# Seven early pieces, prefetched compression weights, full transposes and an output block's first half begun early, in a hybrid attention and RWKV-7 layer on one core

## The chip, the cores and the metric

The kernel runs on one core of one Trainium2 chip. The metric is device time of one execution in microseconds (us), from outside the program; less is better. TensorE (PE) does the matmuls, VectorE (DVE), ScalarE (ACT) and GpSimd (POOL) the elementwise work, SyncE (SP) issues nearly all DMA transfers, in one queue and in program order.

## What is computed

One decoder layer over 256 tokens of width 2048 in float32. The reference, cut to what matters:

```python
hn = rms_norm(h, pre_norm_g)
proj = hn @ w_in                       # 2048 -> q, kv6, gates, z_a, feat_b, z_b
o_a = nsa_mixer(q, k_cmp, v_cmp, k_slc, v_slc, k_win, v_win, gates, ...)
o_b = rwkv7_mixer(feat_b, mu, w0, w2, a0, a2, k_k, k_a, r_k, ln_w, ln_b)
mix = concat([o_a * silu(z_a), o_b * silu(z_b)])
h = h + rms_norm(mix @ w_out, post_norm_g)
# in nsa_mixer: kc = silu(blocks(k_cmp) @ cmp_k_w1) @ cmp_k_w2, the same for v; softmax branches
# in rwkv7_mixer: a recurrence over time with a 64 x 64 state for each of 16 heads, y normalized by head
```

## The kernel before, in words

**Split matmuls.** Every weight is loaded as float32 (SP), rounded to a high part H (ACT, L287), and the rest is kept as a low part L (DVE, L288). A product is three matmuls: H with the high and the low part of the activations, L with the high part. The helper `mm` (L154) issues every matmul and `transpose` (L167) every transpose, so these two lines stand for all of PE's work. Four raw buffers, four H and three L hold the weights on their way.

**Pieces.** The input projection is 57 feature-major pieces, f0 to f56, of 128 output features each: f0 is the low-rank input, then 12 pieces of RWKV half 0 (heads 0 to 7), 8 of keys and values, 12 of RWKV half 1, 8 queries and 16 z. A piece is two halves (f60 and f61 are the halves of piece 6) of 24 matmuls of 128x256. `N_FIRST` = 4 pieces are begun together while x arrives; the pieces from there to `N_EARLY` take a bank of `banks`; from then on each takes one of the two banks of `ppool`. Before the first query stand the token-major pieces, t00 to t15 (`token_major`): two groups w of 96 matmuls of 128x268, each with two PSUM banks `pts`, which ACT empties (L1138, L1139). The output projection has four blocks n of 512 columns and eight pieces j each; a piece o{n}{j} is 12 matmuls of 128x512, for two token halves i. Pieces j = 0 to 3 (the A part) need mixA, the attention's result; j = 4 to 7 (the B part) need mixB, the RWKV result. PSUM has 8 banks: 2 in `ppool`, 6 in `banks`, which all other work shares.

**Order.** The program is written by generators in lanes (chain, rwkv, blk0, blk1, nsa0, nsa1, gate). After each piece `progress` runs every generator that is due by a clock that counts PE's columns (`now`); `yield 9.0` says that the next step is due 9 us of matmuls later. `pick` runs lanes until a buffer is free. The tile scheduler then orders each engine's instructions, with priorities by kind (`level`).

**Steps touched.** `row_statistics` gives the row norm as a broadcast tile `rbc` (matmul `arena,small` 128x256, copy L455); every piece's evacuation (L537) needs it, and the 128x384 matmul after it makes the attention bias rows. `compress` multiplies blocks of keys and values by eight chunks of the compression weights of 512 KB (SP L943, L947), each loaded one chunk ahead; its matmuls are those of 128x32. `solve` inverts 32x32 triangles on DVE (L737, L739), sends the result through DRAM (`zs`, `zt`, L745 to L766) and uses it in the 32x32 matmuls after `yield 9.0`. The chain of a half then runs four steps c over 64 tokens: matmuls `VS,GR` and `AR`, a copy on ACT (L824), matmuls 64x64 with the inverse, a copy on DVE (L834), and matmuls for y and the next state; y goes out by ACT (L878). At its end y is normalized (L888 to L894), transposed by eight sets of four 64x64 transposes for both halves, and added to mixB's input by L904. `out_part` computes a part of an output block; the A parts of n = 0 to 2 (`NA` = 3) go out to y2 by ACT (L1249), and the B part is added to that. Block 3 runs all eight pieces at the end:

```python
    for n in range(NA):
        pts = out_part(n, range(4), ppool if n % 2 == 0 else banks)
...
    until(lambda: not any(lanes.values()))
...
    for n in range(4):
        js = list(range(4, 8) if n < NA else range(8))
```

Of the kernel before, what the change touches and what calls it, by code (L numbers as in the profile page):

```python
# [14 lines left out]
ALU = mybir.AluOpType  # L15
# [41 lines left out]
N_EARLY = 6  # L57
# [15 lines left out]
GLAT = 1.5  # L73

# [45 lines left out]
def hybrid_block(ctx: ExitStack, tc: tile.TileContext, xT, xtok, wfm, wtm, wout, vecs, gpost, lora, table,  # L120
# [44 lines left out]
    def transpose(o, i, idn):  # L165
        now[0] += 0.11
        PE.transpose(out=o, in_=i, identity=idn)  # L167
# [132 lines left out]
    for n, j in [(n, j) for n in range(NA) for j in range(4)] + [  # L300
            (n, j) for n in range(4) for j in range(4 if n < NA else 0, 8)]:
        queue.append((wout[n, j], [P, 2, 512], f"o{n}{j}_"))
# [410 lines left out]
    def solve(hb):  # L713
# [53 lines left out]
        yield 9.0  # L767
# [129 lines left out]
        for i in range(4):  # L897
            m = 4 * hb + i
            q0 = 64 * (i % 2)
            ytp = yield from bank()  # L900
            for c in range(4):
                o = T * c + P * (i // 2)
                transpose(ytp[:, 64 * c:64 * c + 64], ysb[q0:q0 + 64, o:o + P], ident[q0:q0 + 64, q0:q0 + 64])
            DVE.scalar_tensor_tensor(mix[1][:, m, :], ytp[:, :T], vcol(V_LNW, m), mix[1][:, m, :], op0=ALU.mult,  # L904
                                     op1=ALU.add)
            ytp.free(2.0)
            yield 0.5
# [15 lines left out]

    def compress(a, nm):
        if a == 0:
            pace(SP.dma_start(post, pos), marks[-2])
            pace(SP.dma_start(w2t, cw2), marks[-2])
        blks = yield from sb(4)
# [9 lines left out]
        w1n = None  # L938
        for hf in range(4):
            w1 = w1n  # L940
            if w1 is None:
                w1 = yield from sb(4)
                pace(SP.dma_start(w1[:], cw1[a, :, 8 * hf:8 * hf + 8, :].rearrange("p j d -> p (j d)")), marks[-2])  # L943
                yield 3.0
            if hf < 3:
                w1n = yield from sb(4)
                pace(SP.dma_start(w1n[:], cw1[a, :, 8 * hf + 8:8 * hf + 16, :].rearrange("p j d -> p (j d)")),  # L947
                     marks[-1])
            for j in range(2):
                for q in range(4):  # L950
                    jj = 4 * j + q
                    mm(cps[32 * q:32 * q + 32, 0:P], blk[:, 8 * hf + jj].rearrange("p g i -> p (g i)"),
                       w1[:, jj * P:jj * P + P], start=hf == 0 and j == 0, stop=hf == 3 and j == 1)
            w1.free(1.0)
            yield 2.0
# [162 lines left out]
    def token_major():  # L1118
        VV = N_.VV = pick(arena, 4).ap.rearrange("p (w i t) -> p w i t", w=2, i=2)
        for w in range(2):  # L1120
            pts = [pick(ppool, 1) for i in range(2)]
# [112 lines left out]
    def out_part(n, js, pool, order=None):  # L1234
        pts = [pick(pool, 1) for i in range(2)]
        for pair in order or [[j] for j in js]:
            hl = [take() for j in pair]
            for i in range(2):
                with at("proj"):
                    for j, (H, L) in zip(pair, hl):  # L1240
                        out_mms(pts[i][:], i, H, L, j, j == js[0], j == js[-1])
            progress()
        return pts

    for n in range(NA):
        pts = out_part(n, range(4), ppool if n % 2 == 0 else banks)
        with at("evac"):
            for i in range(2):
                ACT.activation(y2[:, i, 512 * n:512 * n + 512], pts[i][:], AF.Copy)  # L1249
                pts[i].free(1.0)  # L1250
    until(lambda: not any(lanes.values()))
# [46 lines left out]
    for n in range(4):  # L1298
        js = list(range(4, 8) if n < NA else range(8))
# [6 lines left out]
        pts = out_part(n, js, ppool if n % 2 == 0 else banks, order)  # L1306
# [85 lines left out]
```

## Time and profile before

| | before |
|---|---|
| time, median of 3 runs | 577.52 us (576.17 to 577.62) |
| profiled execution, its own time | 575.76 us |
| its span, first to last instruction | 574.0 us |
| PE busy | 557.3 us (97%), 4812 matmuls |
| weight loads (PEld) | 519.4 us (90%) |
| DVE busy | 426.7 us (74%) |
| ACT busy | 311.8 us (54%) |
| POOL busy | 55.8 us (10%) |
| mean granted clock of TensorE | 0.996 |
| moved by DMA | 99.97 MB, mean 174 GB/s |

The span lies inside the execution's own time; 1.76 us lie around it. A duration in a row of the timeline is from the start of the first instruction to the end of the last; matmuls overlap, so the time that one costs is the distance between two starts. "Idle before" names what the engine waited for last.

### The profile page before, as it was taken

Reading aid. Unit: us, or ns where it says so; the run is one execution under the profiler, and the core shown is the slowest. Engines: PE = TensorE matmul, PEld = TensorE weight load, DVE = VectorE, ACT = ScalarE, POOL = GpSimd, SP = SyncE. Lnnn points to the kernel's source line nnn. Section 1 sums busy time; section 2 is a strip of 40 time slices with the busy share of each in tenths; the row PEclk is TensorE's granted clock in tenths of the full one; section 3 lists DMA queues with packets and bytes.
Section 4 is the critical chain, followed back from the end, with each engine's and each line's share of the span. In section 5 each row is a group of like instructions: output and inputs, shape, how many; then the busy total and the mean of one; then the engine's idle time right before and its main releaser. Section 6 shows DMA issues by size and latency. Waiting matters only on the chain.

```text
span 574.0 us, 12180 instructions
## 1 busy us (share of the span) xinstructions
PE 557.3 (97%) x4812; PEld 519.4 (90%) x4812; DVE 426.7 (74%) x892; ACT 311.8 (54%) x566; POOL 55.8 (10%) x95
## 2 busy tenths in 40 slices
PE   9999999999999999999999999999999999999994
PEld 8998999998989999999988999999999987777883
DVE  5888997867988666569789369899766473576855
ACT  6858764623445434457675468566633353564632
POOL 3202300400000000141031000000000000000002
PEclk9999999999999999999999999999999999999998
DMA  8967444557675844333346253356634455674723
GB/s 293 367 199 248 148 163 140 189 156 237 215 268 154 214 145 148 121 114 104 99 138 212 95 156 120 120 167 209 186 114 146 136 158 188 185 293 153 227 90 147
DMA packets 41365, 99.97 MB, mean 174 GB/s; under 512 B 14395, under 2 KB 17116, under 8 KB 40924
## 3 DMA queue, kind: packets, MB, share of 16 engines
q1 hardware_dynamic: 41020, 98.88, 53.2%
q8 instruction: 38, 0.62, 0.5%
q10 hardware_dynamic: 288, 0.31, 0.2%
q14 instruction: 19, 0.16, 0.1%
HBM read 93.93 MB, written 5.24 MB: 173 GB/s over the span
## 4 chain that ended last, share of the span: by engine, by line
PE 78%; DMA 7%; DVE 5%; ACT 4%; issue 2%; SPq 1%; POOL 1%; DVEq 0%; ACTq 0%
PE banks L154 76%; PE banks L167 2%; DMA arena<-in_cw_dram 2%; DMA us<-GR 1%; DMA arena<-us 1%; DMA rf__96<-in_wfm_dram 1%; DMA rf__2334<-in_wfm_dram 1%; DMA zs<-arena 1%; DMA arena<-zt 1%; DVE y L1289 0%; SPq L724 0%; DVE small L537 0%; ACT arena L1036 0%; ACT L892 0%; POOL arena L627 0%
## 5 line engine op out<-in xcount | busy, mean ns | idle before, releaser
L154 PE MATMUL banks<-arena 128*32 128x128 f32 (+3 forms) x470 | 32.3, 255 | 2.1 <-POOL arena L269 1.1
L154 PEld LDWEIGHTS banks<-arena 128*32 128x32 f32 (+3 forms) x470 | 26.6, 137 | 5.7 <-DMA arena<-in_cw_dram 1.5
L737 DVE TENSOR_TENSOR arena<-arena 64x31 f32<-64x31 f32 (+15 forms) x62 | 20.5, 330 | 8.0 <-DMA arena<-us 7.3
L539 ACT ACTIVATE small<-small 128x256 f32<-128x256 f32 x25 | 12.4, 503 | 17.2 <-DVE small L537 17.1
L739 DVE TENSOR_TENSOR arena<-arena 64x31 f32<-64x31 f32 (+15 forms) x62 | 20.4, 330 | 0.8
L167 PE MATMUL banks<-small,arena 128*128 128x128 f32 (+1 forms) x112 | 16.8, 263 | 0.1
L1094 ACT ACTIVATE arena<-arena 128x256 f32<-128x256 f32 x16 | 6.6, 415 | 18.2 <-DVE arena L1208 15.0
L154 PE MATMUL banks<-AR,arena 64*128 64x128 f32 x128 | 15.4, 289 | 0.0
L154 PEld LDWEIGHTS banks<-AR,arena 64*128 64x128 f32 x128 | 12.2, 187 | 2.4 <-issue 0.5
L167 PEld LDWEIGHTS banks<-small,arena 128*128 128x128 f32 (+1 forms) x112 | 11.8, 139 | 2.6 <-issue 1.1
L594 DVE RECIPROCAL arena<-arena 128x256 f32<-128x256 f32 x8 | 13.8, 1739 | 0.4 <-ACT arena L591 0.2
L1036 ACT ACTIVATE arena<-arena,mx 128x128 f32<-128x128 f32 (+1 forms) x32 | 14.1, 442 | 0.0
L627 POOL TENSOR_SCALAR arena<-arena,small 128x256 f32<-128x256 f32 x8 | 9.8, 1220 | 42.7 <-DVE small L537 34.9
L624 POOL TENSOR_SCALAR arena<-arena 128x256 f32<-128x256 f32 x8 | 9.5, 1187 | 38.8 <-ACT arena L623 37.6
L540 DVE SCALAR_TENSOR_TENSOR arena<-small 128x256 f32<-128x256 f32 x25 | 11.8, 481 | 1.9 <-ACT small L539 1.9
L1293 POOL TENSOR_TENSOR y<-y,xres 128x512 f32<-128x512 f32 x2 | 2.9, 1454 | 101.5 <-ACT y L1292 101.5
L154 PE MATMUL banks<-VS,GR 128*64 128x64 f32 x256 | 11.4, 228 | 0.0
L154 PEld LDWEIGHTS banks<-VS,GR 128*64 128x64 f32 x256 | 9.5, 137 | 1.8 <-issue 0.7
L687 DVE TENSOR_TENSOR GR<-banks,small 128x1024 f32<-128x1024 f32 x8 | 9.8, 1221 | 0.9 <-PE banks L154 0.9
L537 DVE TENSOR_TENSOR small<-banks,small 128x256 f32<-128x256 f32 x25 | 10.3, 417 | 0.2
L1032 DVE CUSTOM_DVE_ANT_0 arena<-banks,arena 128x128 f32<-128x128 f32 (+1 forms) x32 | 10.1, 348 | 0.0
L864 POOL TENSOR_TENSOR arena<-arena,PC 128x256 f32<-128x256 f32 x4 | 2.7, 685 | 71.5 <-DVE arena L854 36.3
(1375 smaller groups left out, 2143.4 us busy)
## 6 DMA issues: line engine op xcount, KB each, us to landing
arena<-in_cw_dram SPq DMA_DIRECT2D x8, 512.0 KB, 4.7
arena<-in_wfm_dram SPq DMA_DIRECT2D x4, 512.0 KB, 8.9
xres<-in_xtok_dram SPq DMA_DIRECT2D x2, 1024.0 KB, 7.5
xr<-in_xT_dram SPq DMA_DIRECT2D x3, 512.0 KB, 7.2
bscr<-arena SPq DMA_DIRECT2D x1, 1536.0 KB
out_dram<-y SPq DMA_DIRECT2D x5, 256.0 KB, 2.3
arena<-bscr SPq DMA_DIRECT2D x8, 128.0 KB, 3.2
gpt<-in_gpost_dram SPq DMA_DIRECT2D x1, 1024.0 KB, 5.0
```

What stands on the lines that cost most here:

```text
L154: last[0] = PE.matmul(o, lhsT, rhs, **kw)
L167: PE.transpose(out=o, in_=i, identity=idn)
L537: DVE.tensor_tensor(f[:, 1:T + 1], pt[:, :T], rbc, op=ALU.mult)
L539: ACT.activation(tm, f[:, 0:T], AF.Copy, scale=vcol(V_MU, c))
L540: DVE.scalar_tensor_tensor(o, f[:, 1:T + 1], omu[:, c:c + 1], tm, op0=ALU.mult, op1=ALU.add)
L594: pace(DVE.reciprocal(A.nrm[i + j], A.nrm[i + j]))
L627: POOL.tensor_scalar(fk[:], ta[:], ka2[:, m:m + 1], ka1[:, m:m + 1], op0=ALU.mult, op1=ALU.add)
L687: DVE.tensor_tensor(A.GR[:, i].rearrange("p h c t -> p (h c) t"), gp.ap.rearrange("p h (c t) -> p (h c) t", c=4), gmask[:, None, :].to_bro ...
L737: DVE.tensor_tensor(t_, U[:, 0:j, j:j + 1].to_broadcast([64, j, w]), Z[:, j:j + 1, j:32].to_broadcast([64, j, w]), op=ALU.mult)
L739: DVE.tensor_tensor(Z[:, 0:j, j:32], Z[:, 0:j, j:32], t_, op=ALU.add)
L1032: DVE.tensor_tensor_reduce(out=dst, in0=src, in1=bb, scale=1.0, scalar=-3.0e38, op0=ALU.add, op1=ALU.max, accum_out=mx[:, i, j:j + 1])
L1036: ACT.activation(dst, dst, AF.Exp, bias=mx[:, i, j:j + 1], accum_out=sm[:, i, j:j + 1])
```

## The change

1. `N_EARLY` goes from 6 to 7: piece 6 takes a bank of `banks` too and may begin before the row statistics are done.
2. The compression weights are fetched by `fetch_cw`, up to two chunks ahead of the one in use, if four arena units and twelve in all are free; each step yields `CWLAT` = 2.5 in place of 3.0 and 2.0.
3. `yield 9.0` before the 32x32 matmuls of `solve` becomes `yield 11.0`.
4. y is transposed by four sets of four 128x128 transposes (two sets for each half) in place of eight sets of 64x64; two instructions per set (now L908) read the bank with a stride.
5. A group of token-major pieces takes one bank of `ppool` and one of `banks`, in place of both of `ppool`.
6. The order of the output weights is: the A parts of all four blocks, then the B parts. The A parts of n = 1 and 2 run in `banks`; that of n = 3 runs in `ppool` and stays there (`held`) until its B part is added at the end, in the same accumulation. All other B parts run in `banks`.

The diff, with the lines that only follow left out:

```diff
-N_EARLY = 6
+N_EARLY = 7
...
+CWLAT = 2.5
...
-    for n, j in [(n, j) for n in range(NA) for j in range(4)] + [
-            (n, j) for n in range(4) for j in range(4 if n < NA else 0, 8)]:
+    for n, j in [(n, j) for js in (range(4), range(4, 8)) for n in range(4) for j in js]:
         queue.append((wout[n, j], [P, 2, 512], f"o{n}{j}_"))
...
-        yield 9.0
+        yield 11.0
         t2p = yield from bank2()
...
-        for i in range(4):
-            m = 4 * hb + i
-            q0 = 64 * (i % 2)
+        for a in range(2):
+
             ytp = yield from bank()
             for c in range(4):
-                o = T * c + P * (i // 2)
-                transpose(ytp[:, 64 * c:64 * c + 64], ysb[q0:q0 + 64, o:o + P], ident[q0:q0 + 64, q0:q0 + 64])
-            DVE.scalar_tensor_tensor(mix[1][:, m, :], ytp[:, :T], vcol(V_LNW, m), mix[1][:, m, :], op0=ALU.mult,
-                                     op1=ALU.add)
+                o = T * c + P * a
+                transpose(ytp[:, P * c:P * c + P], ysb[:, o:o + P], ident)
+            ytv = ytp.ap.rearrange("p (c b t) -> p c b t", c=4, b=2)
+            for b in range(2):
+                m = 4 * hb + 2 * a + b
+                mv = mix[1][:, m, :].rearrange("p (c t) -> p c t", c=4)
+                DVE.scalar_tensor_tensor(mv, ytv[:, :, b, :], vcol(V_LNW, m), mv, op0=ALU.mult, op1=ALU.add)
...
+    cws, cwn = {}, [0]
+
+    def fetch_cw(upto, must):
+
+        while cwn[0] < upto and arena.find(4) is not None and (must or arena.busy.count(False) >= 12):
+            n = cwn[0]
+            cws[n] = arena.take(4)
+            cwn[0] += 1
+            pace(SP.dma_start(cws[n][:], cw1[n // 4, :, 8 * (n % 4):8 * (n % 4) + 8, :].rearrange("p j d -> p (j d)")),
+                 marks[-2])
...
+            fetch_cw(2, False)
...
+            n = 4 * a + hf
+            fetch_cw(min(n + 3, 8), False)
+            if n not in cws:
+                yield lambda: arena.find(4) is not None
+                fetch_cw(n + 1, True)
+                yield 4.0
+            w1 = cws.pop(n)
...
-            yield 2.0
+            yield CWLAT
...
-            pts = [pick(ppool, 1) for i in range(2)]
+            pts = [pick(pool, 1) for pool in (ppool, banks)]
...
-    def out_part(n, js, pool, order=None):
-        pts = [pick(pool, 1) for i in range(2)]
+    def out_part(n, js, pool, order=None, begun=None):
+        pts = begun or [pick(pool, 1) for i in range(2)]
...
-                        out_mms(pts[i][:], i, H, L, j, j == js[0], j == js[-1])
+                        out_mms(pts[i][:], i, H, L, j, not begun and j == js[0], n < NA and j == js[-1] or j == 7)
...
-        pts = out_part(n, range(4), ppool if n % 2 == 0 else banks)
+        pts = out_part(n, range(4), ppool if n == 0 else banks)
...
+    held = out_part(NA, range(4), ppool)
     until(lambda: not any(lanes.values()))
...
-        js = list(range(4, 8) if n < NA else range(8))
+        js = list(range(4, 8))
...
-        pts = out_part(n, js, ppool if n % 2 == 0 else banks, order)
+        pts = out_part(n, js, banks, order, held if n == NA else None)
```

In the program as it is built, `mm` is now L156, `transpose` L169, the casts L289 and L290, the copies of the chain L825 and L835, y's way out L879.

**On PE, at the row statistics.** Names: hf51 and lf51 are the H and L parts of the second half of piece 5; `arena,small` 128x256 is the broadcast of `rbc`, 128x384 the bias rows. Before:

```order
L154 MATMUL banks_74<-xH_76,lf51__475 128x256 x8
L154 MATMUL banks_74<-arena_73,small_72 128x256
L154 MATMUL banks_74<-arena_73,small_72 128x384
L154 MATMUL banks_74<-xH_76,hf60__506 128x256
L154 MATMUL banks_74<-xL_75,hf60__506 128x256
```

Of the change:

```order
L156 MATMUL banks_74<-xH_76,lf51__475 128x256 x8
L156 MATMUL banks_74<-xH_76,hf60__506 128x256
L156 MATMUL banks_74<-xL_75,hf60__506 128x256
...
L156 MATMUL banks_74<-arena_73,small_72 128x256
...
L156 MATMUL banks_74<-xH_76,lf60__505 128x256 x8
L156 MATMUL banks_74<-xH_76,hf61__547 128x256
...
L156 MATMUL banks_74<-arena_73,small_72 128x384
```

Twelve matmuls of f60 now stand ahead of the broadcast, and the rest of f60 and twelve of f61 between it and the 128x384.

**On SP, at the compression weights.** `in_cw1` is a chunk of them, rf180 the raw weights of the first half of piece 18, `us0` the way of `solve` through DRAM. Before:

```order
L943 DMA arena_73<-in_cw1_dram 128x1024
L279 DMA rf180__1492<-in_wfm_dram 128x1024
L279 DMA rf181__1540<-in_wfm_dram 128x1024
L279 DMA rf190__1581<-in_wfm_dram 128x1024
L947 DMA arena_73<-in_cw1_dram 128x1024
L724 DMA us0_1522<-GR0_742 32x16x32 x4
L279 DMA rf191__1629<-in_wfm_dram 128x1024
L730 DMA arena_73<-us0_1522 64x1024
L947 DMA arena_73<-in_cw1_dram 128x1024
```

Of the change:

```order
L281 DMA rf180__1519<-in_wfm_dram 128x1024
L935 DMA arena_73<-in_cw1_dram 128x1024
L281 DMA rf181__1561<-in_wfm_dram 128x1024
L935 DMA arena_73<-in_cw1_dram 128x1024
L281 DMA rf190__1604<-in_wfm_dram 128x1024
L281 DMA rf191__1648<-in_wfm_dram 128x1024
L935 DMA arena_73<-in_cw1_dram 128x1024 x2
L725 DMA us0_1502<-GR0_742 32x16x32 x4
L935 DMA arena_73<-in_cw1_dram 128x1024
```

The second chunk's load moves ahead from behind rf190 to behind rf181, and the third, fourth and fifth are issued by the time at which the third was.

**On PE, at the end of the A parts.** ho13 and lo13 are the last A piece of n = 1, `arena` 64x64 the product with the inverse in step c = 3 of half 1, which L824 (L825) must have copied for and which L834 (L835) copies out. Before:

```order
L154 MATMUL banks_74<-VS1_3330,GR1_3329 64x64 x8
L154 MATMUL banks_74<-arena_73,AR1_3328 64x128 x4
L154 MATMUL banks_74<-ho10__5821,mixA_5769 128x512 x4
...
L154 MATMUL banks_74<-ho13__5925,mixA_5769 128x512 x3
L154 MATMUL banks_74<-arena_73 64x64 x8
L154 MATMUL banks_74<-ho13__5925,mixA_5769 128x512
```

Of the change:

```order
L156 MATMUL banks_74<-ho13__5904,mixA_5734 128x512 x4
L156 MATMUL banks_74<-lo13__5903,mixA_5734 128x512 x2
L156 MATMUL banks_74<-VS1_3348,GR1_3347 64x64 x8
L156 MATMUL banks_74<-arena_73,AR1_3346 64x128 x4
L156 MATMUL banks_74<-arena_73 64x64 x8
L156 MATMUL banks_74<-VS1_3348,GR1_3347 64x64 x8
L156 MATMUL banks_74<-arena_73,AR1_3346 64x128 x4
L156 MATMUL banks_74<-ho20__5935,mixA_5734 128x512 x4
```

Before, 21 output matmuls stood between the chain's AR matmuls and the 64x64 that needs their result, and others behind it; now the three chain steps follow each other directly.

## Rows read from the trace of the kernel before

**Rows 1.** Waits of PE: line waited for, us in total, times, longest.
```profile
PE banks L154 <- ACT small L1139: 2.5, 2, 1.4
...
PE banks L154 <- DMA arena<-in_cw_dram: 1.0, 1, 1.0
PE banks L154 <- DMA arena<-zt: 0.7, 1, 0.7
```

**Rows 2.** The page: busy time of the engines, landing of the compression weights' loads.
```profile
PE 557.3 (97%) x4812; PEld 519.4 (90%) x4812; DVE 426.7 (74%) x892; ACT 311.8 (54%) x566; POOL 55.8 (10%) x95
...
arena<-in_cw_dram SPq DMA_DIRECT2D x8, 512.0 KB, 4.7
```

**Rows 3.** Busy time in stretches: us; PE, PEld, DVE, ACT, POOL busy; clock; DMA.
```profile
60.00:80.00 20.00, 19.89 (x172) 19.52 (x171) 19.77 (x35) 14.46 (x23) 4.32 (x6) 1.00 0.44 149
...
566.00:574.00 8.00, 0.00 (x0) 0.00 (x0) 4.46 (x8) 1.51 (x4) 1.47 (x1) 0.72 0.57 213
```

**Rows 4.** Timeline of PE and DVE at the row statistics: start, us, engine, line.
```profile
42.42 0.59 PE L154 MATMUL banks<-arena,small 128*128 128x256 f32 x2
44.23 0.59 PE L154 MATMUL banks<-arena,small 33*128 33x384 f32 x1 [1.22 <-DVE small L455]
...
43.76 0.42 DVE L455 COPY small<-banks 128x256 f32<-128x256 f32 x1
```

**Rows 5.** Timeline of PE at the first wait for compression weights.
```profile
132.66 0.75 PE L154 MATMUL banks<-xH,lf__1460 128*128 128x256 f32 x5
134.41 0.43 PE L154 MATMUL banks<-arena 128*32 128x128 f32 x8 [0.99 <-DMA arena<-in_cw_dram]
```

**Rows 6.** Timeline of SP and PE from half 0's inverse to its first use.
```profile
183.83 0.47 SPq L745 DMA_DIRECT2D zs<-arena  x1
...
195.45 1.43 SPq L766 DMA_DIRECT2D arena<-zt  x3
...
197.74 0.24 PE L154 MATMUL banks<-arena,GR 32*32 32x32 f32 x2 [0.67 <-DMA arena<-zt]
```

**Rows 7.** Timeline of PE at the first wait of the token-major pieces.
```profile
292.42 0.28 PE L154 MATMUL banks<-KCL,qh 128*128 128x256 f32 x1
293.87 0.39 PE L154 MATMUL banks<-ht__3305,xH 128*128 128x268 f32 x1 [1.17 <-ACT small L1139]
```

**Rows 8.** Timeline of PE at the first output piece.
```profile
468.22 0.50 PE L154 MATMUL banks<-ho__5627,mixA 128*128 128x512 f32 x1
469.38 0.83 PE L154 MATMUL banks<-ho__5627,mixA 128*128 128x512 f32 x2 [0.66 <-DVE arena L1208]
```

**Rows 9.** Timeline of PE: one set of 64x64 transposes, one of 128x128, what follows.
```profile
511.48 0.46 PE L167 MATMUL banks<-small,arena 64*128 64x64 f32 x4
511.87 1.20 PE L154 MATMUL banks<-ho__6059,mixB 128*128 128x512 f32 x4
...
305.83 0.60 PE L167 MATMUL banks<-small,arena 128*128 128x128 f32 x4
306.36 1.16 PE L154 MATMUL banks<-AR,arena 64*128 64x128 f32 x16
```

**Rows 10.** Timeline of PE, ACT and DVE: one chain step of half 1 among output pieces.
```profile
488.55 0.66 PE L154 MATMUL banks<-arena,AR 128*64 128x128 f32 x8
489.14 1.19 PE L154 MATMUL banks<-ho__5821,mixA 128*128 128x512 f32 x4
...
494.12 0.73 PE L154 MATMUL banks<-arena 64*64 64x64 f32 x16
494.78 0.50 PE L154 MATMUL banks<-ho__5925,mixA 128*128 128x512 f32 x1
...
489.29 0.39 ACT L824 ACTIVATE arena<-banks 128x256 f32<-128x256 f32 x1 [2.80 <-PE banks L154]
491.79 1.06 ACT L287 ACTIVATE ho__5983<-ro__5980 128x1024 fp32r<-128x1024 f32 x1 [0.36 <-PE banks L154]
...
494.89 0.68 DVE L834 COPY VS<-banks 64x512 f32<-64x512 f32 x1
```

More of the change, by code (lines that the diff above doesn't have):

```diff
@@ L937, in compress @@
         cps = yield from bank()
-        w1n = None
         for hf in range(4):
[L940 to L948, printed above, removed]
+            n = 4 * a + hf
[5 more added lines that the diff above has]
+            w1 = cws.pop(n)
             for j in range(2):
```

## The prediction

> **What bounds the kernel now.** I read the page first: PE is busy 557.3 us of a span of 574.0, no other engine over 427 [rows 2]. So the time is PE's work plus the places where PE stands. The stretches come next: the last 8 us hold no matmul [rows 3], and that tail (norm, product and way out of the last block) is not touched. This leaves 574.0 - 557.3 - 8.0 = 8.7 us in which PE stands between its first and its last matmul. The list of waits then says for whom: 2.5 us for ACT's emptying of the token-major banks, 1.0 for compression weights, 0.7 for the reads of zt [rows 1], 1.2 for the copy of rbc [rows 4], 0.7 before the first output piece [rows 8]; about 2.6 us are small and have no name there. The timelines give the size of each place, because a wait costs more than its idle time: the five matmuls ahead of the compression take 0.75 us, one alone 0.28 [rows 5, 7], so they follow each other every (0.75 - 0.28)/4 = 0.12 us. By that step the sixth would have started at 133.26, and it started at 134.41: 1.15 us lost, where 0.99 are called idle. I add 0.16 us for each wait. An output matmul of 128x512 steps by (1.20 - 0.50)/3 = 0.23 us [rows 8, 9].
>
> So the change can win by taking waits away (7 us at most, with these additions) or by taking work from PE, and it can lose by making new waits. DVE matters wherever it is full: from 60 to 80 us it is busy 19.77 of 20 us while PE is busy 19.89 [rows 3].
>
> **The change part by part.**
>
> *Seventh early piece.* Before, PE goes straight from the broadcast to the 128x384 and waits 1.22 us for L455, which DVE finishes at 43.76 + 0.42 [rows 4]. Now 12 matmuls of f60 (1.44 us) stand ahead of the broadcast and 24 others (2.9 us) between it and the 128x384, more than the wait. Gain 1.22 + 0.16 = 1.4 us. What is late next: rbc itself, by up to 1.4 us, and every L537 behind it on DVE. These empty the piece banks, and with a seventh piece six of the six banks are taken at that moment (two of the first four pieces, three early ones, the one of the statistics). DVE has a quarter of a microsecond to spare from 60 to 80, so the other end is 0.
>
> *Compression weights.* A load of a chunk lands after 4.7 us [rows 2]; it was issued one chunk ahead and PE waited at the first [rows 5]. Now the second chunk is issued right behind the first piece of raw weights that follows the first chunk, and three more a little later. Gain 1.15 us, I take 1.2 with the small second place. The chunks are passed by none that PE waits for: on SP the raw weights rf190 and rf191 and the way of `solve` (us0) now stand behind one or two chunks more, issues of about half a microsecond each [rows 6]; at the other end one of them is late by one load and the gain is 0.
>
> *The inverse of `solve`.* zs is issued at 183.83 and the product starts at 197.74, 13.9 us later, behind reads of zt that are issued until 196.9 [rows 6]. The later yield moves the product from the second half of f27 to the first of f30. But zs too is now issued later: it stood behind raw load rf280 with the product in f271, it now stands behind rf301 with the product in f300. Raw loads run ahead of PE by a fixed number of buffers, so in both orders the distance is one half-piece less than that lead, and the wait stays. I take 0; ends are -0.9 us (gone) and +0.7 (doubled).
>
> *Token-major pieces.* Group w = 1 began when ACT had emptied both banks of w = 0, and the first query when it had emptied w = 1: two waits, 2.5 us [rows 1], the first of 1.17 [rows 7]. With a bank of each kind, each next user finds a free one, and the emptying has a whole group of 96 matmuls (11.5 us) to hide under. Gain 2.5 + 2 x 0.16 = 2.8 us. For it all others have one bank fewer of six for two groups; RWKV half 1 and the heads behind it move later and press on DVE there. Bound from the nearest row: one such wait comes back, 1.5 us; the other end is 2.8.
>
> *First output piece.* It loses 469.38 - 468.22 - 0.23 = 0.93 us, waiting for the last head's work on DVE [rows 8]. In the new order two more sets of 64x64 matmuls of the chain stand ahead of it, 0.66 us each, from 494.12 to 494.78 [rows 10]. The splits of mixA still end last, so I take 0.6; ends 0 and 0.9.
>
> *Full transposes.* A set of four 64x64 takes 0.39 us to the next matmul, one of four 128x128 takes 0.53 [rows 9]. Eight of the first are 3.1 us, four of the second 2.1: at least 1.0, at most 1.5 if the large ones step like the small. I take 1.2. L908 reads as many elements with a stride; it follows PE and hides under output matmuls.
> By the Trainium skill, TensorEngine Tiling (Array Packing), Key Properties, different tiles "can execute LdWeights and Matmul in parallel". By that rule the small transposes, which alternate between the two halves of the partitions, would overlap and the full ones would win nothing; the sum below would be 1.2 us smaller. The row speaks against it: four small ones take 0.39 us, 0.10 each, one behind the other [rows 9].
>
> *Order of the output parts.* The A part of block 3 only moves: 4 x 12 matmuls, 11 us, from the end to ahead of the first B matmul, where they cover half 1's norm and gate. No wait there is in the list now, so the gain is 0. The norm of y had 42 output matmuls as cover before its first transposes and has 36 now, 8.3 us; it had no wait, so the cost is 0, at the other end the 6 matmuls, 1.4 us.
>
> *A new wait.* At the end of block 1's A part the chain's AR, the 64x64 and VS,GR now follow each other with nothing between. The step as it ran before: AR at 488.55, the next matmul at 489.14, L824 from 489.29 for 0.39 [rows 10]. The 64x64 can start at about 489.7, so PE stands 0.6 us. The 64x64 take until 494.78, L834 runs from 494.89 for 0.68, so VS,GR waits until 495.6: 0.8 us more. Cost 1.4 us. ACT also has a weight cast of 1.06 us in its queue [rows 10]; if that and a half of its like on DVE are in the way, it is 3.2. It can hardly be less than 1.2.
>
> Sum: -1.4 - 1.2 + 0 - 2.8 - 0.6 - 1.2 + 1.4 = -5.8 us. The profiled execution took 575.76 us (span 574.0 and 1.76 around it) and would take 570.0. It lies 1.76 us under the median of the runs, 577.52, so the median should come to **571.7**.
>
> **The rivals.**
> *All waits go.* zt's wait too (0.9), the first piece's whole (0.3 more), transposes at 1.5, the new wait at 1.2, and half of the 2.6 us without a name: -5.8 - 0.9 - 0.3 - 0.3 - 0.2 - 1.3 = -8.8, 568.7 us. For it: PE has nothing else to wait for. Against it: the distance of zs.
> *DVE gives it back.* The gain at 44 us returns as waits for L537 (1.4), one token-major wait returns further down (1.5), the new wait is 3.2 (1.8 more): -5.8 + 4.7 = -1.1, 576.4 us. For it: DVE is full from 60 to 80 us. Against it: PE is full there as well, so it carries the load.
> *Slower: the chain of half 1 runs in the open.* It ran beside the last projection pieces and now falls deeper into the A parts, with three steps c there. If each of them, not only the last, waits for its two copies at the upper price of 3.2 us, that is 9.6 in place of 1.4: -5.8 + 8.2 = +2.4, 579.9 us. It decides at the point where the copies L825 stand behind a cast that itself waits for its raw load. Against it: in the new order output matmuls stand between the steps of c = 1 and c = 2.
> *Part of the change does nothing.* Full transposes win nothing because small ones overlap: 572.9.
>
> **How the numbers follow.** The forecast has a chance of 0.55; all waits gone 0.15; DVE gives back 0.18; the open chain 0.08; no gain by the transposes 0.04. A measurement of this kernel can tell 0.3%, 1.7 us, from no change: faster is under 575.8, slower over 579.3. Faster holds the forecast, the first rival, the last and a third of the second: 0.80; same the rest of the second: 0.12; slower 0.08. The range reaches from 568.0, a little under the best case, to 576.5, at the second rival; above it lie the open chain and a part of the second.
>
> **What would show it.** In the list of waits L455, in_cw and L1139 are gone and zt stays. Output matmuls at the end of block 1 show two idle gaps, one behind the copy L825 and one behind L835, 0.6 and 0.8 us. L169 has 16 fewer transposes and PE's busy time falls by about 1 us. The tail stays at 8 us. I am wrong if PE shows waits for L537 between 45 and 80 us, if RWKV or the heads wait for a bank from 280 us on, or if PE stands before the first B matmul.

## The result, and the profile after

The changed kernel takes **571.64 us** (median of 4 runs, 571.08 to 572.24); before, in the same session, 577.48 (576.17 to 577.62). The ratio is 0.9904, with a 95% interval of 0.9886 to 0.9923: faster by about 1%, some 5.5 us. The profiled execution is the shortest of the four, 571.08 us, with a span of 569.3. One execution further down, the profiled one of e9, ran at a granted clock of 0.85 from end to end; its lengths are not used.

The page of the kernel after, busy time of the engines:

```profile
PE 552.2 (97%) x4796; PEld 519.2 (91%) x4796; DVE 426.8 (75%) x892; ACT 311.1 (55%) x566; POOL 57.2 (10%) x95
```

PE's busy time fell by 5.1 us [rows 2], far more than the 1 us that I had ascribed to the transposes, though in this execution part of PE's work ran slower than before. The list of waits of PE after (line waited for; us in total, times, longest), beside [rows 1]:

```profile
PE banks L156 <- DMA arena<-zt: 2.7, 1, 2.7
...
PE banks L156 <- DMA arena<-in_cw_dram: 1.0, 2, 0.6
PE banks L156 <- DVE VS L835: 0.8, 1, 0.8
PE banks L156 <- ACT KT L664: 0.7, 1, 0.7
...
PE banks L169 <- DVE arena L655: 0.5, 1, 0.5
PE banks L156 <- ACT arena L825: 0.5, 1, 0.5
```

Gone are the row statistics, both token-major waits and the first output piece. The compression weights are still there, and the wait for zt is four times as long. L835 and L825 are the new wait that was forecast; L664 and L655 were not in the forecast.

**The reads of zt.** Timeline of SP and PE of the kernel after, beside [rows 6]:

```profile
206.75 0.35 SPq L281 DMA_DIRECT2D rf__2582<-in_wfm_dram  x1
207.14 1.91 SPq L767 DMA_DIRECT2D arena<-zt  x4
...
209.73 0.28 PE L156 MATMUL banks<-xH,hf__2436 128*128 128x256 f32 x1
212.68 0.31 PE L156 MATMUL banks<-arena,GR 32*32 32x32 f32 x2 [2.67 <-DMA arena<-zt]
```

The matmul at 209.73 would have been followed after 0.12 us, so 2.83 us are lost; before it was 0.83. The two matmuls at 212.68 need only the first of the four reads (the other 62 of the product follow 0.8 us later). This read, from issue to landing, in the chains of work that ended last, before and after:

```profile
193.54 4.16 DMA arena<-zt
...
207.14 5.50 DMA arena<-zt
```

Before, it was issued 3.4 us ahead of the place at which PE wanted it (196.91), now 2.7 us ahead of it (209.85), and it lands 1.3 us later behind its issue: together the 2.0 us by which the wait grew. And that is not all. Busy time in stretches of the kernel after (us; PE, PEld, DVE, ACT, POOL busy; granted clock; DMA share, GB/s):

```profile
212.70:215.00 2.30, 2.30 (x66) 1.95 (x67) 0.15 (x1) 0.00 (x0) 0.00 (x0) 0.50 0.72 278
...
219.00:220.00 1.00, 1.00 (x10) 1.00 (x10) 0.37 (x1) 0.00 (x0) 0.00 (x0) 0.97 0.00 0
```

PE stood for 2.67 us, and behind that it ran at a granted clock of 0.50, the level of 1.2 GHz in place of 2.4, until 219.05. PE counts as busy all that time. The matmuls themselves show the price (timeline of PE after):

```profile
215.13 0.41 PE L156 MATMUL banks<-xL,hf__2436 128*128 128x256 f32 x1
215.34 0.41 PE L156 MATMUL banks<-xH,hf__2436 128*128 128x256 f32 x1
```

They start 0.21 us apart where 0.12 is usual. Summed over the 85 matmuls from 212.7 to 219.05 this costs 3.2 us, so the place lost 6.0 us, where it had lost 0.83.

**The end of the A parts.** Timeline of PE after, beside [rows 10]:

```profile
490.77 0.66 PE L156 MATMUL banks<-arena,AR 128*64 128x128 f32 x8
491.90 0.73 PE L156 MATMUL banks<-arena 64*64 64x64 f32 x16 [0.47 <-ACT arena L825]
493.47 0.73 PE L156 MATMUL banks<-VS,GR 128*64 128x64 f32 x16 [0.84 <-DVE VS L835]
```

Two gaps in the places that were forecast, 0.69 and 1.02 us lost by distance of starts.

**Where the 4.7 us are.** The last matmul starts at 565.38 before and at 560.70 after; the rest is the same tail, again 8 us without a matmul. For every matmul of both timelines I took the distance to the next start and subtracted the median distance of its kind over both traces. What is left, in us:

| left over | before | after |
|---|---|---|
| places that lost over 0.3 us | 8.7 (9 places) | 9.5 (11) |
| the stretch at the low clock | 0 | 3.2 |
| changes of the tile's shape, as from 128x128 to 32x32 | 13.7 (127) | 10.1 (92) |
| other changes of kind, shape the same | -2.0 (272) | -2.9 (280) |
| steps within one kind, under 0.3 us | 7.4 | 3.3 |

With 0.2 us less pure work this is -4.7 us. How finely kinds are told apart moves one to three microseconds between the last two rows and the work (with the tiles' names told apart the last row is 8.7 and 6.0); the first three rows hardly move. So the named waits, on which most of my sum rested, grew by 0.8 us in total; the gain is in the last three rows, of which my sum held only the transposes.

### The profile page after: what moved, and what is told of

It reads as the page before. It is cut to its first block, busy times and chain, and to the rows that moved or that the text cites. A ratio compares the mean times of both kernels' runs of the same rounds, so it can differ in the third digit from the quotient of the medians.

```text
span 569.3 us, 12190 instructions
## 1 busy us (share of the span) xinstructions
PE 552.2 (97%) x4796; PEld 519.2 (91%) x4796; DVE 426.8 (75%) x892; ACT 311.1 (55%) x566; POOL 57.2 (10%) x95
## 4 chain that ended last, share of the span: by engine, by line
PE 83%; DMA 7%; DVE 4%; ACT 2%; issue 1%; POOL 1%; SPq 1%; DVEq 0%; ACTq 0%; POOLq 0%
PE banks L156 81%; PE banks L169 2%; DMA arena<-zt 2%; DMA arena<-us 1%; DMA rf__96<-in_wfm_dram 1%; DMA rf__5253<-in_wfm_dram 1%; DMA us<-GR 1%; DMA rf__3609<-in_wfm_dram 1%; DMA arena<-in_cw_dram 1%; POOL arena L628 1%; DVE y L1303 0%; DMA arena<-zs 0%; SPq L725 0%; DVE arena L949 0%; DVE arena L738 0%
## 5 line engine op out<-in xcount | busy, mean ns | idle before, releaser
L156 PE MATMUL banks<-arena 128*32 128x128 f32 (+3 forms) x470 | 30.2, 251 | 2.5 <-POOL arena L271 1.1
L156 PEld LDWEIGHTS banks<-arena 128*32 128x32 f32 (+3 forms) x470 | 25.9, 134 | 6.0 <-DMA arena<-in_cw_dram 1.7
L169 PE MATMUL banks<-small,arena 128*128 128x128 f32 x96 | 15.8, 274 | 0.5 <-DVE arena L655 0.5
L156 PE MATMUL banks<-AR,arena 64*128 64x128 f32 x128 | 14.9, 287 | 0.7 <-ACT KT L664 0.7
L156 PEld LDWEIGHTS banks<-AR,arena 64*128 64x128 f32 x128 | 12.1, 187 | 2.9 <-issue 1.8
L1048 ACT ACTIVATE arena<-arena,mx 128x256 f32<-128x256 f32 (+1 forms) x32 | 14.1, 443 | 0.0
L169 PEld LDWEIGHTS banks<-small,arena 128*128 128x128 f32 x96 | 11.3, 140 | 1.3 <-DVE arena L655 0.7
L156 PE MATMUL banks<-VS,GR 128*64 128x64 f32 x256 | 11.4, 228 | 0.8 <-DVE VS L835 0.8
L156 PEld LDWEIGHTS banks<-VS,GR 128*64 128x64 f32 x256 | 9.6, 137 | 2.6 <-DVE VS L835 1.0
L861 POOL MEMSET arena<- 64x256 f32 x12 | 3.7, 308 | 65.0 <-DVE arena L1107 36.7
L1044 DVE CUSTOM_DVE_ANT_0 arena<-banks,arena 128x256 f32<-128x256 f32 (+1 forms) x32 | 10.2, 349 | 0.0
L625 POOL TENSOR_SCALAR arena<-arena 128x256 f32<-128x256 f32 x8 | 8.1, 1014 | 18.0 <-ACT arena L624 17.9
```

Source lines behind the costliest of these rows:

```text
L156: last[0] = PE.matmul(o, lhsT, rhs, **kw)
L1044: DVE.tensor_tensor_reduce(out=dst, in0=src, in1=bb, scale=1.0, scalar=-3.0e38, op0=ALU.add, op1=ALU.max, accum_out=mx[:, i, j:j + 1])
L1048: ACT.activation(dst, dst, AF.Exp, bias=mx[:, i, j:j + 1], accum_out=sm[:, i, j:j + 1])
```

## Experiments

All runs were compared with the kernel before on the same chip; it took 576.3 to 576.4 us in the later sessions. The question was first why the change won no more: the trace above says that the late reads of zt, with the low clock behind them, give back over 5 us of a gain that is larger than my sum. Each expectation names its own theories.

**e1: the product of `solve` later, half 0 alone.**

```diff
-        yield 11.0
+        yield 7.0
+        old = tc.cur_priority
+        if hb == 0:
+            tc.cur_priority = level["proj"]
```

(and the old priority again behind the product)

> The kernel after the change, with the 32x32 product of half 0's inverse placed by program order among the projection pieces, two half-pieces later (its first matmul stands in f310, not in f300), so that the reads of zt have landed. Theory A (the wait for zt costs its 2.8 us and, behind it, some 6 us of matmuls at the lower of the two clock levels, 3.1 us more): no wait for zt, granted clock 1.00 throughout, 571.6 - 5.9 = 565.7 us. Rival B (the low clock has another cause and stays): 568.8 us. Rival C (the chain of half 0, which is now later, gives it back further down): 571 us.

Measured: 575.62 us (574.68 to 580.15), ratio 1.0002 [0.9978, 1.0026]. Waits of PE in e1:

```profile
PE banks L169 <- DVE arena L655: 2.6, 2, 2.1
PE banks L156 <- ACT KT L664: 2.6, 2, 1.5
PE banks L156 <- ACT arena L624: 2.4, 2, 1.8
```

The wait for zt is gone, and 7.6 us of waits for ACT and DVE stand elsewhere, nearly all between 294 and 322 us. From 319.55 to 326.38 the clock is again 0.50; it fell 0.2 us into the longest of these waits (319.35 to 321.48), 2.4 us behind the end of one of 1.8 us. The whole order moved with the one product, so this run can't price zt.

**e2: keep PE at work during the wait.** Six more matmuls of 32x256 ahead of the product; they go into a bank that the product then overwrites, and only add work.

```diff
+        for q in range(6 if hb == 0 else 0):
+            mm(t2p[0:32, 0, 0:T].rearrange("p (j t) -> p j t", t=32), ZT[64:96, 0, 0, :], ZT[64:96, :, 0, :], start=True, stop=True)
```

> The kernel after the change, with six more matmuls of 32x256 (some 2.6 us of PE work whose result is overwritten) between the pieces and the product with the inverse, which wait for the first of the four reads of zt and not for the last. The product itself can start no earlier than before. Theory A (the clock falls because PE stands still for 2.8 us): the idle stretch is cut to about 1 us, the clock stays at 1.00 behind it, 571.6 - 3.1 = 568.5 us or a little more. Rival B (the low clock has another cause): 571.6 us, with the same 6 us at half clock.

Measured: 574.43 us (571.62 to 576.43), ratio 0.9964 [0.9944, 0.9985]. Timeline of PE in e2:

```profile
212.85 2.38 PE L156 MATMUL banks<-arena 32*32 32x256 f32 x9 [2.81 <-DMA arena<-zt]
```

The added matmuls read zt themselves, and its four reads land within 0.5 us of each other, so they waited too, and the low clock came behind that wait as before. The run tells nothing of what it was made for; 2.8 us is what it cost.

**e3: the small transposes again.** The part of the diff on the transposes of y undone, which was point 4 of the change.

```diff
-                transpose(ytp[:, P * c:P * c + P], ysb[:, o:o + P], ident)
+                transpose(ytp[:, 64 * c:64 * c + 64], ysb[q0:q0 + 64, o:o + P], ident[q0:q0 + 64, q0:q0 + 64])
```

> The kernel after the change with the 64x64 transposes of y put back, all else as after. Theory A (a set of four 64x64 costs 0.39 us and its entry, eight sets against four): 571.6 + 1.3 = 572.9 us. Rival (small transposes overlap, so full ones win nothing): 571.6 us.

Measured: 580.96 us (580.11 to 581.55), ratio 1.0091 [1.0075, 1.0107]. Waits of PE in e3:

```profile
PE banks L169 <- ACT arena L1065: 1.9, 1, 1.9
PE banks L156 <- DVE arena L905: 1.5, 1, 1.5
```

Those two are new, with 1.0 each for L1042 and L1078. They are in the attention heads and before the first B part, and a low clock stands behind the first: the planner's order changed far from the transposes. Most of the 9.3 us is the order's, not theirs. How the small transposes run, alone and two sets together, is seen in this trace:

```profile
524.17 0.47 PE L169 MATMUL banks<-small,arena 64*128 64x64 f32 x8
...
529.03 0.46 PE L169 MATMUL banks<-small,arena 64*128 64x64 f32 x4
```

Eight take as long as four. The eight are two sets, one of each half of the partitions, and they start in pairs 0.01 us apart. A set alone lies in one half, and its four start 0.11 and 0.06 us apart.

**e4: both token-major banks from `ppool` again.**

```diff
-            pts = [pick(pool, 1) for pool in (ppool, banks)]
+            pts = [pick(ppool, 1) for i in range(2)]
```

> The kernel after the change with both banks of a token-major group taken from the piece banks again, all else as after. Theory A (two waits for ACT's emptying come back, 2.8 us, and the 0.85 us that PE now waits for ACT's copy of KT behind the same emptying goes): 571.6 + 2.0 = 573.6 us. Rival (the sixth bank is worth as much to the others as the waits cost): 571.6 us.

Measured: 575.51 us (572.41 to 578.27), ratio 0.9994 [0.9970, 1.0018]. Waits of PE in e4:

```profile
PE banks L156 <- ACT small L1151: 4.1, 1, 4.1
```

Busy time and clock (the number behind POOL's) of e4 behind this wait, which ended at 289.99:

```profile
290.00:292.00 2.00, 2.00 (x11) 2.00 (x12) 0.00 (x0) 1.22 (x3) 0.00 (x0) 0.65 0.77 266
```

The wait for the emptying comes back, as one of 4.1 us, and once more the clock falls behind it. The part is worth at least its term.

**e5: the product of `solve` at its place in the program, both halves.**

```diff
-        yield 11.0
+        yield 5.0
...
+        with at("proj"):
+            for i in range(4):
```

> The kernel after the change with the 32x32 products of the inverse of both halves placed by program order among the pieces (yield 5.0 ahead of them): for half 0 one half-piece later than after, in f301, all 32 together. Theory A (the wait for zt and the matmuls at the lower clock behind it cost 5.9 us, and a new order elsewhere costs what its own waits cost): no wait for zt of over 1 us, clock 1.00 behind it, 571.6 - 5.9 = 565.7 us if the other waits stay as they are. Rival C (whatever is later in half 0's chain gives it back, as in the first trial of this kind): 574 to 576 us.

Measured: 565.77 us (565.64 to 565.80), ratio 0.9819 [0.9800, 0.9838]. The mean clock is 0.997 (after: 0.989) and no wait for zt is left; SP and PE in e5:

```profile
207.95 1.91 SPq L767 DMA_DIRECT2D arena<-zt  x4
...
215.59 0.93 PE L156 MATMUL banks<-arena,GR 32*32 32x32 f32 x64
```

The reads are issued no earlier than after (207.14); the product comes 5.7 us later than its place there, 209.85. The time is under the changed kernel's by 5.9 us, or 4.9 if each is taken by its ratio to before; the place had lost 6.0 by the accounting above.

**e6 and e7: e5 with the compression weights three chunks ahead**, and one constant of the planner's clock changed in each as well (GLAT, steps of the chain, or ZLAT, steps of `solve`).

```diff
-GLAT = 1.5
+GLAT = 2.5
...
-            fetch_cw(min(n + 3, 8), False)
+            fetch_cw(min(n + 4, 8), False)
```

> The kernel before this one (products by program order) with compression weights fetched three chunks ahead and the chain's steps due 2.5 us apart in place of 1.5. Theory A (waits are what differs between orders): the two waits for compression weights, 0.8 and 0.5 us, go, the chain's two waits at the end of the A parts shrink: 563 to 565 us. Rival (one chunk more in the queue of SP delays raw weights, and PE waits for these): 566 us or more.

> The products by program order and three chunks ahead, as in the kernel before this one, with the chain's steps as after and the inverse's steps on DVE due 1.2 us apart in place of 1.0. Theory A: the two waits for compression weights go, no new one comes, 563 to 565 us; what it gives above or below the kernel before it is what a new order is worth by itself. Rival (the inverse ends later and PE waits for zt again): 568 us or more, with a wait for zt of over 2 us.

(e7: ZLAT 1.0 to 1.2 in place of GLAT.) Measured: e6 562.40 us (561.73 to 562.82), ratio 0.9761 [0.9737, 0.9785]; e7 **561.75** us (561.18 to 562.01), ratio 0.9748 [0.9729, 0.9768]. The wait for in_cw (2.2 us in e5) is gone in both; the list of waits of e7, whole:

```profile
PE banks L156 <- POOL arena L271: 1.1, 1, 1.1
PE banks L169 <- DVE arena L655: 0.5, 1, 0.5
```

So the change's two chunks ahead were one too few. The two kernels are 3.4 and 4.0 us under e5, more than the 2.2: the order moved too, and e5's wait of 1.2 us for L1021 is gone as well. e7 beats both kernels, the one before by 2.5% and the changed one (by the ratios) by 1.6%, and is the base of e9 to e11.

**e8: the changed kernel with a yield of 9.0**, part 3 of the change undone and nothing else.

```diff
-        yield 11.0
+        yield 9.0
```

> The kernel after the change with the yield ahead of the 32x32 products back at 9.0: nothing else. Theory A (the scheduler places the product by its own idea of when zt lands, so the yield hardly moves it; a wait of 2.8 us or a little more and the low clock stay): 571.6 us, and within 2 us of it by other waits in the new order. Rival (the yield of 11.0 is what made the wait grow from 0.7 to 2.7 us): the wait is 1 us or less, no low clock, 567 us.

Measured: 566.34 us (564.80 to 567.81), ratio 0.9829 [0.9801, 0.9857]. It is the rival's number. SP and PE in e8:

```profile
204.51 0.45 SPq L767 DMA_DIRECT2D arena<-zt  x1
205.06 0.40 SPq L281 DMA_DIRECT2D rf__2582<-in_wfm_dram  x1
205.50 1.42 SPq L767 DMA_DIRECT2D arena<-zt  x3
...
207.69 0.24 PE L156 MATMUL banks<-arena,GR 32*32 32x32 f32 x2
```

The product is wanted 2.2 us earlier than after, and there is no wait: one read of zt goes out ahead of the raw load rf__2582, where after all four stood behind it. Before, too, one read went ahead (SP of the kernel before):

```profile
193.54 0.30 SPq L766 DMA_DIRECT2D arena<-zt  x1
193.94 1.47 SPq L279 DMA_DIRECT2D rf__2401<-in_wfm_dram  x1
```

So the later yield, which puts the product later, cost 5.3 us (4.3 by the ratios): it moved the first read by as much as the product (2.6 and 2.2 us) and behind a load of 512 KB. The order moved elsewhere too (PE waits 1.8 us for compression weights in e8, 1.0 after, and not for L835, L825 or L664), so this is the price of the two orders and not of the one wait alone. But e5, where the reads stay late and the product waits for them among other work, and e8, where the first read is early, agree: without the zt trouble the change wins about 10 us, where my sum had 5.8, or 6.7 with zt's whole 0.9.

**e9: e7 with the small transposes.** The edit is that of e3.

> Base: the kernel of e7 (561.75 us). Alone undone: the full transposes of y; the 64 x 64 ones in alternate row groups stand again. Theory A (the term of 1.2 us is sound, and the 8.0 us too much of e3 came from waits of its new order): 563.0 to 563.6, PE busy more by about 1 us, no new wait over 0.5 us on PE. Rival (the small transposes ran beside other work, so nothing was won): 561.8, within 0.3%. If again a new wait of 1 us or more stands on PE, the order decides and the term can't be read from the time.

Measured: 565.2 us (three executions, 565.06 to 566.37), ratio 0.9815 [0.9794, 0.9837]; 3.5 us more than e7, and more than theory A had. The order of e9 has six sets alone and two sets together. At the prices worked out below from the other traces (0.60 us for a set alone or two together, 0.44 for a full one) these are 4.2 us in place of 1.8, so 2.4 of the 3.5 us are the transposes. The other 1.1 us stand in an order that moved, and no run splits them further. The rival, that nothing was won, is out for this order, in which six of eight sets stand alone.

**e10: e7 with both token-major banks from `ppool`.** The edit is that of e4.

> Base: the kernel of e7 (561.75 us). Alone undone: the second kind of banks for the token-major pieces; all again come from ppool. Theory A (the term of 2.8 us: two waits for the emptying behind L1139, now L1151, come back): 564.5 or more, with one or more waits on small of L1151 that sum to 2 us or more. Rival (the waits only stand there when the banks were late for another reason): 561.8 and no such wait.

Measured: 567.33 us (566.86 to 568.24), ratio 0.9848 [0.9830, 0.9866], 5.6 us more than e7. Timeline of PE in e10:

```profile
300.91 0.39 PE L156 MATMUL banks<-xH,hf__3567 128*128 128x256 f32 x1 [3.35 <-ACT small L1152]
```

Busy time and clock of e10 behind the second wait:

```profile
303.00:306.00 3.00, 3.00 (x17) 3.00 (x16) 1.47 (x2) 2.43 (x9) 0.61 (x2) 0.52 0.00 0
```

Theory A holds: two waits for the emptying (L1152 here), 3.6 us in sum by the list, this one 3.4, and the low clock. A wait of 1.2 us for L574 at 279 us is new as well, so not all of the 5.6 us is the part's price.

**e11: e7 with six early pieces.**

```diff
-N_EARLY = 7
+N_EARLY = 6
```

> Base: the kernel of e7 (561.75 us). Alone undone: the seventh early piece; six stand again. Theory A (the term of 1.4 us: the second output of the row statistics waits for rbc): 562.9 to 563.5, with a wait of 1 us or more for the row statistics near 42 us. Rival (the statistics' chain is over by then): 561.8 and no such wait.

Measured: 564.08 us (563.83 to 564.76), ratio 0.9794 [0.9774, 0.9813], 2.3 us more than e7. Timeline of PE in e11:

```profile
43.99 0.91 PE L156 MATMUL banks<-arena,small 33*128 33x384 f32 x2 [1.22 <-DVE small L456]
...
140.90 0.41 PE L156 MATMUL banks<-yhkc,small 128*128 128x32 f32 x2 [1.35 <-DVE yhkc L981]
```

The first is the wait of [rows 4] to the hundredth, at 1.4 us lost. The second, in the compression, is the new order's and makes up the rest, less the wait for L655, which is gone. Term right, time over its range by 0.6 us.

**e12: the changed kernel with the old output order**, part 6 undone. Up to the end of the A part of block 1 (4436 matmuls) PE's order is that of the changed kernel.

```diff
-    held = out_part(NA, range(4), ppool)
...
-        js = list(range(4, 8))
+        js = list(range(4, 8) if n < NA else range(8))
```

> Base: the changed kernel (571.64 us). Alone undone: the held A part of the fourth output block and the pools that go with it; all pieces up to the end of block 1 keep their order. Theory A (the two waits for VS and for the cast behind L825 and L835, 0.65 and 0.96 us, come of the chain of half 1 losing its cover of an A part): both go, 570.0 to 570.6, less what a short wait before the first B part takes back (0.2 to 0.3). Rival (the held A part gives cover at the first output piece that is lost again): a wait of 0.9 us or more stands before the first B part and the time is 571.6 to 573.

Measured: 571.45 us (567.93 to 574.45), ratio 0.9905 [0.9874, 0.9936], no different from the changed kernel. Timeline of PE in e12:

```profile
493.84 0.73 PE L156 MATMUL banks<-VS,GR 128*64 128x64 f32 x16
...
507.59 1.90 PE L156 MATMUL banks<-ho__6043,mixB 128*128 128x512 f32 x7 [0.38 <-ACT mixB L1118]
...
514.49 0.66 PE L169 MATMUL banks<-small,arena 128*128 128x128 f32 x4 [0.24 <-DVE arena L896]
515.62 0.74 PE L156 MATMUL banks<-lo__6154,mixB 128*128 128x512 f32 x2 [0.48 <-DVE lo__6154 L290]
```

Each theory is half right. The two chain waits are gone, as A said; in their place PE waits before the first B matmul, before a transpose of y and for a weight's low part, 0.60 + 0.40 + 0.64 us lost. From the last common matmul to the last start it is 71.47 us; in the changed kernel it is 70.77: in these two executions the held A part wins 0.7. The execution shown is the longest of eight. Its wait for zt is 3.5 us in place of 2.7, in the same order, and its clock fell once more, at 119 us (last section). The runs of this one kernel go with the clock: 567.93 us at 0.997, 572.4 to 574.5 at 0.989.

## Why the prediction was right, and where it was not

The forecast was 571.7 us, the result is 571.64, and it is right for partly wrong reasons: one term was wrong by 5.2 us, another by 1.4, and a gain of some 7 us was not in the sum. That they cancel is luck. From profile to profile the kernel won 4.7 us (575.76 to 571.08) where the sum had 5.8; the medians meet the forecast to 0.1 us because the profiled execution of the kernel before lay 1.8 us under its median and that of the changed one 0.6. By the sum's own steps, from distances of starts:

| step | forecast | measured |
|---|---|---|
| seventh early piece | -1.4 | -1.5; e11 brings the wait back |
| compression weights | -1.2 | +0.2 |
| reads of zt | 0 (-0.9 to +0.7) | +5.2 |
| token-major banks | -2.8 | -2.9; e10 brings 3.6 back |
| first output piece | -0.6 | -0.9 |
| transposes | -1.2 | -3.0 |
| order of the output, norm | 0 | no new wait of the norm; see e12 |
| new wait at the end of block 1 | +1.4 | +1.7 |
| waits not in the forecast | | +2.1 |
| shape changes, without the transposes | | -3.0 |
| other steps under 0.3 us: what is left | | -2.6 |

**zt, the wrong step.** I had argued that raw loads run ahead of PE by a fixed number of buffers, "so in both orders the distance is one half-piece less than that lead, and the wait stays". The distance of zs to the product was indeed about the same (183.83 to 196.91, the place at which PE wanted it, is 13.1 us before; 197.01 to 209.85 is 12.8). But the last leg decided: the first read of zt was issued 3.4 us ahead of its place in the kernel before, and 2.7 us in the changed one, right behind a raw load, where it took 5.5 us to land and not 4.2. I had the row with x3 reads [rows 6] and did not ask where the fourth stood. And even a right stall would have been priced at 2.8 us: that a stall of this length is followed by 6.3 us at half the clock I did not have.

**Compression weights.** The wait at the first chunk did not go: it lost 1.15 us before and 0.80 after, and a new one of 0.59 stands at a later chunk:

```profile
133.75 1.08 PE L156 MATMUL banks<-arena 128*32 128x128 f32 x32 [0.64 <-DMA arena<-in_cw_dram]
...
148.14 0.28 PE L156 MATMUL banks<-xL,hf__1688 128*128 128x256 f32 x1
148.35 1.08 PE L156 MATMUL banks<-arena 128*32 128x128 f32 x32
149.75 0.64 PE L156 MATMUL banks<-arena 128*32 128x128 f32 x16 [0.32 <-DMA arena<-in_cw_dram]
150.32 0.38 PE L156 MATMUL banks<-xH,hf__1688 128*128 128x256 f32 x1
150.55 0.28 PE L156 MATMUL banks<-xL,hf__1688 128*128 128x256 f32 x1
```

The planner now takes two chunks' matmuls together (x32, 16 each), so a chunk's lead is used up by the pairing, and the load takes 5.2 us to land where 4.7 was my price [rows 2]. e6 and e7 show that a third chunk takes the wait away.

**The gain without a name** is in those rows too. From the piece to the 128x32 matmuls it is 0.21 us where 0.12 is a step: about 0.1 us for a change of the tile's shape. And on the way back the first matmul of the piece (150.32) is followed only after 0.23 us: 0.1 us more. This second part is counted in the row of steps within one kind; it sums to 6.6 us before and 4.5 after, so it makes 2.1 us of that row's gain. The two timelines have 131 changes of shape before (127 of them without a longer wait) and 99 after, with 80 rows or columns counted as 128. Sixteen of the 32 are the entries and exits of the 64x64 transposes; e3 and e9, which put these back, have 16 more changes than their bases (115 and 113, where 99 and 97 stood). The other sixteen come of sets that run together, 3.0 us. Between kinds of the same shape there is no price (-0.01 us each). By the Trainium skill, TensorEngine Tiling (Array Packing), Key Properties, changing the tiling mode drains the TensorE; the rows agree, at 0.1 to 0.2 us. That fewer shape changes come of the merging, I argue from counts; no run changed that alone. The 2.6 us in other small steps I can't name, and they are hardly a property of the change: in e8 the row of steps within one kind is 9.6 us, where it is 8.7 before and 6.0 after.

**Transposes.** I had priced a small set from its first start to the next matmul, 0.39 us, without its entry and without the slow first matmul behind it; with both it is 0.60 us. The full set that I priced at 0.53 us [rows 9] stood ahead of 64-row matmuls, so a change of shape was in its price. A set for y in the changed kernel:

```profile
502.88 0.60 PE L169 MATMUL banks<-small,arena 128*128 128x128 f32 x4
503.23 0.48 PE L156 MATMUL banks<-ho__5993,mixA 128*128 128x512 f32 x1
```

It takes 0.35 us, and 0.44 with the matmul behind it. Eight at 0.60 less four at 0.44 are 3.0 us. I had also dismissed the rule of the Trainium skill, TensorEngine Tiling (Array Packing), Key Properties, that different tiles work in parallel, by the row of four that run one behind the other [rows 9]. That row can't test it: the four of a set lie in the same half of the partitions, and only the next set lies in the other. Where two sets ran together (e3), the eight took as long as four (0.47 and 0.46 us), so this trace agrees with the rule; in the kernel before every set stood alone, so it did not apply, and the full ones won.

**The new wait** was sized well. It is 0.69 and 1.02 us, where 0.6 and 0.8 were forecast; L825 stood behind a copy of y on ACT (L1261, 0.58 us), not behind the weight cast of the upper bound. What I did not see is that the old order would have had waits of its own in its place (e12), so in these two executions the order of the output wins 0.7 us, where by my terms it lost 0.8 (1.4 for the new wait less 0.6 at the first output piece).

**Waits not in the forecast.** I had said that I would be wrong "if RWKV or the heads wait for a bank from 280 us on". One does, L664, 0.84 us. ACT is late there by the very emptying that no longer holds up the token-major pieces, the most of it a load of a function table, 1.28 us (timeline of ACT and PE after):

```profile
300.24 1.28 ACT L1151 ACT_TABLE_LOAD   x1
...
302.21 1.09 ACT L664 ACTIVATE KT<-banks 128x512 f32<-128x512 f32 x2
...
302.96 1.16 PE L156 MATMUL banks<-AR,arena 64*128 64x128 f32 x16 [0.68 <-ACT KT L664]
```

That is the rival "DVE gives it back" in kind, on ACT, at a fifth of its price.

**The idle time without a name** was smaller than I had it. Of the 2.6 us, 1.1 are PE's wait ahead of its first matmul, which starts at 1.07 us in both kernels; I had put all of it between the first and the last, and half of it into the rival in which all waits go.

## What to carry to other kernels

Before you cost a moved wait at nothing, find in the DMA queue the last instruction on which the waiter depends, and what stands right ahead of it: one raw load ahead of a small read decided 5 us here, and a "later" step moved its own data later with it. Where PE will stand for more than a step or two, look in the rows for what it did behind the last stall of that length, since the clock can double the price. Price a small set of matmuls from the matmul ahead of it to the second one behind it, in the place where it will stand. Count changes of tile shape on PE in the new order, too, not only the waits. And where a planner sets the order, one run that undoes one part prices the part only if the list of waits shows no new ones.

## What was not expected of the hardware

Behind long waits of PE the granted clock fell to 0.50: behind 2.67 us in the changed kernel (for 6.3 us of matmuls, costing 3.2), behind 2.4 and 1.87 us in e3, 2.9 and 4.1 us in e4, 3.35 us in e10. Behind the waits of 1.22 and 1.17 us in [rows 4, 7], of 1.35 us in e11 and of 1.57 us in e5 (at 150.80) it stayed at 1.00. But a long wait is not needed. In e12 PE waited 0.52 us for L655 until 116.44, and from 119.25 to 122.66 the clock was 0.50:

```profile
119.30:122.60 3.30, 3.30 (x17) 3.21 (x16) 1.26 (x2) 0.00 (x0) 1.10 (x2) 0.50 0.60 194
```

The changed kernel has the same order there and the same wait (0.51 us), and stayed at 1.00. So the length of one wait does not decide it alone; what else does, no run here shows. The wait for zt, too, differs in one and the same order, 2.7 us in the changed kernel and 3.5 in e12, and the eight runs of e12 lie 6.5 us apart, with clocks from 0.997 to 0.989.
